# Swapped operands in the state-space output products, transposed outputs for the GLU, and an earlier load of the third token tile, in a one-core hybrid encoder step

## The chip, the cores and the metric

The kernel runs on 1 core of one Trainium2 chip. The metric is the device time of one execution in microseconds (us). The time before is 1225.95 us, the median of 3 runs (1225.14 to 1464.7 us).

## The reference

One layer of a streaming encoder runs over 2048 prompt frames (one new stream) and 8 x 16 frames of running streams, that is 17 tiles of 128 tokens with 1024 features, in float32:

```
z = rms_norm(x) @ w_in                      # [u | g_s | q | k | v | g_a], 6 x 512 columns
# state-space branch: 32 groups of 16 channels, each with 64 complex states
h[l] = a * h[l-1] + b @ u[l]
y    = gelu(Re(c @ h) + d * u)              # 512 channels
val, gate = split(y @ w_glu)
y_s  = val * sigmoid(gate)                  # the GLU
# attention branch: 8 heads of 64, own 64-frame chunk and 8 chunks before (prompt),
# or 512 cached frames (running streams)
y_a  = attention(rms_norm(q), rms_norm(k), v)
out  = x + concat[y_s * silu(g_s), y_a * silu(g_a)] @ w_out
```

Outputs are both token blocks, the newest keys and values, and the last states.

## The kernel before, in words

The program is written in an order fixed by hand. A foreground (`inproj`, `glu`, `outproj`) holds the large products; each step of it is one `mm3`: three 128x512 matmuls (high and low halves of split operands, lines 189 to 191) that add into one PSUM tile. After each step the foreground yields a cost, and `run` gives a share of it (`ratio`) as credit to a background (`s5`, then `decode`, then `attention`), whose pieces so fall between the foreground's steps on every engine's queue. Every DMA discussed here is issued by SyncE (SP), whose queue is strictly in order.

`inproj` makes three passes over the 17 tiles (u and k; v and q; the two gates). For each tile, `dma_h` loads the transposed tokens into `xraw`, which has one buffer; `conv_h` turns it into a high part `hhi` on ScalarE (line 228) and a low part `hlo` on VectorE (line 231), and only then is the next `xraw` load issued (line 214). At the start the first two tiles come in quarters (lines 349 to 354), the first 16 weight chunks are converted (`conv_w`), and each conversion issues the load of the weight chunk five ahead into a ring of five buffers (`load_w`, line 139). The third tile is loaded by `dma_h(2)` on line 370, behind all of these.

`s5` works in 8 batches of 4 groups. The tokens are cut into 272 runs of L = 8 positions (256 of the prompt, 16 of the running streams). For each batch, `UT` holds the inputs with (position in the run, channel) on partitions and the 272 runs along the free axis, and `HP` holds the state before each run. `step_b1` makes the state inputs (one 128x272 matmul per group, line 771), VectorE does the rotations and the scan, and `step_c` makes the outputs: for the blocks of 128, 128 and 16 runs it takes `UT` and `HP` as the stationary operand and the matrices `Tm` and `CA` as the moving one (lines 842 and 843, for the small block 849 and 852). The result has runs on partitions; a GELU on ScalarE reorders it, and `step_y` stores it to the DRAM tensor `y_d` (line 862: tokens by channels, three DMAs per batch in pieces of 256 bytes). `build_e` writes the next `Tm` with 8 small DMAs (line 701), and `load_u` loads `U` (line 711).

`glu` reads `y_d` one token tile at a time (`glu_load`, line 1336). `glu_tr` turns it with four transposes on TensorE (line 1344) and makes the high and low parts from PSUM (lines 1347 and 1348); they are the stationary operands of 24 matmuls per tile. The transposes stand in TensorE's queue in the middle of the tile before.

Of the kernel before, what the change touches and what calls it, by code (L numbers as in the profile page):

```python
# [7 lines left out]
F32 = mybir.dt.float32  # L8
# [11 lines left out]
L = 8  # L20
# [15 lines left out]
def rv(ap):  # L36
    return ap.bitcast(F32R)


# [4 lines left out]
class Build:  # L44
# [15 lines left out]
    def consts(self, st):  # L60
# [6 lines left out]
        self.y_d = d.tile([NT * 128, 512], F32, name="y_d")  # L67
# [14 lines left out]

        self.identr = c.tile([128, 128], F32R, name="ident")
        self.ident = fv(self.identr)
        nc.vector.tensor_scalar(self.identr, ip, 0.0, None, op0=OP.is_equal)
# [26 lines left out]
    def open_fg(self, st):  # L112
# [10 lines left out]
        for f in (1, 0):  # L123
            self.chunks += [((3, f, k), I["w_glu"][128 * k:128 * k + 128, 512 * f:512 * f + 512], None) for k in range(4)]
# [17 lines left out]
    def conv_w(self):  # L142
# [50 lines left out]
    def inproj(self):  # L193
# [176 lines left out]
        dma_h(2)  # L370
# [17 lines left out]
        for ps in range(3):  # L388
            for ti, t in enumerate(TILES):
# [5 lines left out]
                for gi in range(2):  # L395
                    g = passes[ps][gi]
                    z = self.psm.tile([128, 512], F32, tag="mm", name="z")
                    for k in range(8):
# [10 lines left out]
                        if ps == 2 and last and gi == 1 and k == 3:  # L409
                            self.glu_tr(TILES[0])  # L410
                            self.glu_load(TILES[1])
# [37 lines left out]
    def s5(self):  # L449
# [254 lines left out]
        y4 = self.y_d.rearrange("(c j) e -> c j e", j=L)  # L704
        BLK = [(0, 128), (128, 128), (256, 16)]
        U, P, UT, HP = {}, {}, {}, {}
# [15 lines left out]
        def step_a(b, i):  # L722
            c0, n = BLK[i]
            if i == 0:
                UT[b] = mp.tile([128, GB, 272], F32, tag="UT", name="UT")
                HP[b] = mp.tile([128, GB, 273], F32, tag="HP", name="HP")
                nc.vector.memset(HP[b][:, :, 0:1], 0.0)
                nc.vector.tensor_copy(HP[b][:, :, 257:273].rearrange("p g (b k) -> p g b k", k=2)[:, :, :, 0],
                                      h0[:, b * GB:(b + 1) * GB, :])
# [4 lines left out]
            nc.scalar.activation(out=UT[b][:, :, c0:c0 + n], in_=p[:, :, 0:n], func=AF.Copy)  # L734
# [39 lines left out]
        def step_swap(b, g):  # L774
            v = VV[b, g]
            vs = mp.tile([128, 256], F32, tag="vs", name="vs")
            nc.scalar.activation(out=vs[0:64], in_=v[64:128, 0:256], func=AF.Copy)
            nc.scalar.activation(out=vs[64:128], in_=v[0:64, 0:256], func=AF.Copy)
            if g == 0:
                SV[b] = mp.tile([128, GB, 2 * NB], F32, tag="sv", name="sv")  # L780
            nc.scalar.activation(out=SV[b][:, g], in_=v[:, 256:272], func=AF.Copy)
            VV[b, g] = v, vs

        def step_rot(b, g):
# [6 lines left out]
            tt(t1, co, v[:, 0:256], op=OP.mult)  # L791
# [12 lines left out]
        def step_h(b, g):  # L804
# [6 lines left out]
            tt(HP[b][:, g, 1:257], t3, t4, op=OP.subtract)  # L811

        def step_fin(b):
# [8 lines left out]
            h1 = HP[b][:, :, 257:273].rearrange("p g (b k) -> p g b k", k=2)[:, :, :, 1]  # L822
# [9 lines left out]
            nc.vector.tensor_copy(FINp[:, gs], HP[b][:, :, 256])  # L832

        def step_c(b, i):
            c0, n = BLK[i]
            p = ps.tile([128, GB, 128], F32, tag="y", name="y", bufs=2)
            y = mp.tile([128, L, GB * CH], F32, tag="y", name="y")
            yg = y[0:n].rearrange("p j (g h) -> p g j h", g=GB)
            ca = [CA[b][:, g, 1:9].rearrange("p j h -> p (j h)") for g in range(GB)]
            if i < 2:  # L840
# [4 lines left out]
            else:  # L845

                o = [p[32 * g:32 * g + n, 0] for g in range(GB)]
                for g in range(GB):
                    nc.tensor.matmul(o[g], UT[b][:, g, c0:c0 + n], Tm[b % 2][:, g], start=True, stop=False,
                                     tile_position=(0, 32 * g))  # L850
                for g in range(GB):
                    nc.tensor.matmul(o[g], HP[b][:, g, 257:257 + n], ca[g], start=False, stop=True,
                                     tile_position=(0, 32 * g))
                for g in range(GB):
                    nc.scalar.activation(out=yg[:, g], in_=o[g].rearrange("p (j h) -> p j h", j=L),
                                         func=AF.Gelu_apprx_tanh)
            YS[b, i] = y
# [16 lines left out]
        for n in range(3):  # L874
# [3 lines left out]
            if n == 0:  # L878
                build_c(0)
# [3 lines left out]
        for b in range(NBATCH):  # L883
            nx = b + 1 < NBATCH
            for sl in range(6):
# [7 lines left out]
                if b and 1 <= sl < 4:  # L893
                    step_y(b - 1, sl - 1)
# [8 lines left out]
                if b and sl < 3:  # L903
                    step_c(b - 1, sl)
# [18 lines left out]
        for i in range(3):  # L923
            step_c(NBATCH - 1, i)
            yield 1740
            step_y(NBATCH - 1, i)
# [680 lines left out]
```

## Time and profile before

| what | value |
| --- | --- |
| median of the runs shown | 1225.95 us |
| the profiled execution's own time | 1226.13 us |
| its span, first to last instruction | 1224.3 us |
| mean granted TensorE clock | 0.995 |
| VectorE busy | 742.6 us (61%) |
| ScalarE busy | 597.7 us (49%) |
| GpSimd busy | 366.6 us (30%) |
| DMA, mean over the span | 193 GB/s, 190119 packets |

The span is cut into stages that overlap: input projection until about 700 us (the state-space branch in its background from about 245 to 585 us, the cached attention until about 670 us), the GLU until about 880 us, and the output projection to the end; band attention runs behind the last two. Matmuls are pipelined, so a matmul's own duration (0.39 us for 128x512) is longer than the step from its start to the next one's; costs on TensorE are read from start to start. In the timeline an `x2` or `x16` counts instructions merged into one row; a product of two plain float32 operands is two instructions.

### The profile page before, as it was taken

How to read it: one execution, taken by the hardware profiler on the slowest of the kernel's cores; microseconds unless marked ns; L12 is line 12 of the kernel's file. 1: busy time of each engine (PE TensorE's matmuls, PEld its weight loads, DVE VectorE, ACT ScalarE, POOL GpSimd, SP SyncE). 2: the span in 40 equal slices, each digit the busy share in tenths (PEclk: the TensorE clock that was granted, in tenths of full speed). 3: DMA queues.
4: the chain of work that ended last, by engine and by line, in shares of the span. 5: the costliest groups of instructions: out<-in, count | busy, mean ns of one | idle time of the engine just before them, and what ended most of it. 6: DMA issues, size and time to landing. Idle time of an engine off the chain costs nothing.

```text
span 1224.3 us, 18936 instructions
## 1 busy us (share of the span) xinstructions
PE 1193.0 (97%) x6687; PEld 983.1 (80%) x6687; DVE 742.6 (61%) x1391; ACT 597.7 (49%) x1159; POOL 366.6 (30%) x455
## 2 busy tenths in 40 slices
PE   8999999899999998999999999999999999999998
PEld 5788888777788876887777878788888888888876
DVE  5324556868999988985444456565565555555511
ACT  6434446266666656553232346565654555455410
POOL 2433242557767735540000011111211121121120
PEclk9999999999999998999999999999999999999999
DMA  8876556655545567433895688897877777767243
GB/s 252 262 250 181 155 177 202 195 142 129 149 123 151 135 195 214 110 93 88 270 382 171 204 247 245 255 265 205 217 221 215 206 240 241 196 205 225 73 136 107
DMA packets 190119, 236.58 MB, mean 193 GB/s; under 512 B 58136, under 2 KB 122656, under 8 KB 189000
## 3 DMA queue, kind: packets, MB, share of 16 engines
q1 hardware_dynamic: 189016, 232.15, 64.2%
q0 software_dynamic: 864, 3.21, 0.8%
q8 instruction: 53, 0.87, 0.3%
q14 instruction: 42, 0.34, 0.1%
q10 hardware_dynamic: 144, 0.00, 0.0%
HBM read 169.48 MB, written 67.80 MB: 194 GB/s over the span
## 4 chain that ended last, share of the span: by engine, by line
PE 78%; DMA 6%; DVE 6%; POOL 3%; ACT 3%; issue 2%; SPq 1%; DVEq 0%; ACTq 0%; POOLq 0%
PE z L189 19%; PE z L191 18%; PE z L190 18%; PE o L1218 6%; PE pt L1200 5%; PE s L1170 5%; DMA wraw<-in_w_in_dram 3%; PE pt L294 1%; PE o L1057 1%; PE y L843 1%; SPq L701 1%; PE y L842 1%; PE v L771 1%; ACT whi L155 1%; PE s L1015 1%
## 5 line engine op out<-in xcount | busy, mean ns | idle before, releaser
L189 PE MATMUL z<-whi,hhi 128*128 128x512 f32 x816 | 339.2, 416 | 1.4 <-ACT whi L155 0.7
L190 PE MATMUL z<-wlo,hhi 128*128 128x512 f32 x816 | 321.3, 394 | 3.3 <-DVE wlo L156 3.1
L191 PE MATMUL z<-whi,hlo 128*128 128x512 f32 x816 | 320.7, 393 | 0.5 <-DVE hlo L231 0.5
L189 PEld LDWEIGHTS z<-whi,hhi 128*128 128x128 f32 x816 | 154.1, 189 | 38.9 <-issue 5.1
L190 PEld LDWEIGHTS z<-wlo,hhi 128*128 128x128 f32 x816 | 154.5, 189 | 36.5 <-DVE wlo L156 8.0
L191 PEld LDWEIGHTS z<-whi,hlo 128*128 128x128 f32 x816 | 154.0, 189 | 34.3 <-DVE hlo L231 1.0
L1207 ACT ACTIVATE pth<-pt 128x640 fp32r<-128x640 f32 (+4 forms) x128 | 81.7, 639 | 129.3 <-PE pt L1200 89.4
L1208 DVE TENSOR_TENSOR ptl<-pt,pth 128x640 fp32r<-128x640 f32 (+4 forms) x128 | 94.6, 739 | 60.6 <-ACT pth L1207 59.7
L189 PE MATMUL z<-whi,mh 128*128 128x512 f32 x272 | 113.7, 418 | 0.0
L1115 POOL MEMSET bias<- 64x64 f32 x32 | 4.7, 146 | 363.5 <-DMA bias<-tl_d 250.0
L1189 ACT ACTIVATE sn<-sn,mn 128x640 f32<-128x640 f32 (+4 forms) x128 | 96.9, 757 | 29.5 <-DVE mn L1180 29.4
L191 PE MATMUL z<-whi,ml 128*128 128x512 f32 x272 | 107.1, 394 | 1.3 <-POOL ml L1415 1.3
L190 PE MATMUL z<-wlo,mh 128*128 128x512 f32 x272 | 106.7, 392 | 0.0
L1180 DVE CUSTOM_DVE_ANT_0 sn<-s,bias 128x640 f32<-128x640 f32 (+4 forms) x128 | 93.3, 729 | 11.4 <-PE s L1170 10.4
L1170 PE MATMUL s<-ks,q 128*128 128x320 f32 (+1 forms) x448 | 87.4, 311 | 0.0
L1200 PE MATMUL pt<-ident,sn 128*128 128x128 f32 x560 | 83.0, 274 | 3.9 <-DVE ptl L1208 3.1
L1170 PEld LDWEIGHTS s<-ks,q 128*128 128x128 f32 x448 | 74.7, 188 | 11.1 <-DVE mn L1180 1.2
L1200 PEld LDWEIGHTS pt<-ident,sn 128*128 128x128 f32 x560 | 64.9, 140 | 22.5 <-ACT sn L1189 10.0
L231 DVE TENSOR_TENSOR hlo<-xraw,hhi 128x1024 fp32r<-128x1024 f32 x49 | 60.9, 1242 | 20.7 <-ACT hhi L228 20.6
L280 POOL TENSOR_SCALAR s<-s 128x8 f32<-128x8 f32 x34 | 15.9, 468 | 182.9 <-DVE s L279 182.3
L1228 DVE TENSOR_TENSOR ot<-o,tmp 64x512 f32<-64x512 f32 x32 | 22.0, 689 | 74.5 <-ACT tmp L1226 74.5
L191 PEld LDWEIGHTS z<-whi,ml 128*128 128x128 f32 x272 | 51.0, 188 | 13.2 <-POOL ml L1415 1.7
(268 smaller groups left out, 2171.3 us busy)
## 6 DMA issues: line engine op xcount, KB each, us to landing
xraw<-in_xT_dram SPq DMA_DIRECT2D x49, 512.0 KB, 4.5
q<-qt_d SPq DMA_DIRECT2D x64, 256.0 KB, 8.6
ks<-kt_d SPq DMA_DIRECT2D x28, 512.0 KB, 5.6
vhl<-vp_d SPq DMA_DIRECT2D x28, 512.0 KB, 6.7
wraw<-in_w_in_dram SPq DMA_DIRECT2D x48, 256.0 KB, 4.5
bias<-tl_d SPq DMA_DIRECT2D x32, 320.0 KB, 6.3
mt<-mt_d SPq DMA_DIRECT2D x17, 512.0 KB, 7.4
x<-in_x_dram SPq DMA_DIRECT2D x34, 256.0 KB, 5.8
```

The lines of the kernel that those rows point to most:

```text
L189: mm(z, a, whi, start=first, stop=False)
L190: mm(z, a, wlo, start=False, stop=False)
L191: mm(z, b, whi, start=False, stop=last)
L231: nc.vector.tensor_sub(lo, raw, fv(hi))
L1170: nc.tensor.matmul(ps_s[:, bank, 0:wp], Q[n, x2][:, s, 128 * a:128 * a + 128], KS[n][:, s, c0:c0 + wp], start=(x2 == 0), stop=(x2 == 1))
L1180: nc.vector.tensor_tensor_reduce(out=o, in0=i0, in1=i1, scale=1.0, scalar=3e38, op0=OP.add, op1=OP.min, accum_out=mn)
L1189: nc.scalar.activation(out=sn[:, 0:w], in_=sn[:, 0:w], func=AF.Exp, scale=-1.0, bias=mn, accum_out=SUM[n][:, a, s:s + 1])
L1200: nc.tensor.transpose(t[:, k], pr[:, 128 * k:128 * k + 128], self.ident)
L1207: nc.scalar.activation(out=h, in_=t[:, 0:w], func=AF.Copy)
L1208: post.append(lambda: nc.vector.tensor_tensor(out=l, in0=t[:, 0:w], in1=fv(h), op=OP.subtract))
L1218: nc.tensor.matmul(o[:, a0:a1], VB[n][:, j, s, :], t[:, 3 * a0 + j + a0:4 * (a1 - 1) + j + 1:4], start=(y == 0 and j == 4), stop=(y == 1 a ...
L1228: post.append(lambda: nc.vector.tensor_tensor(out=ot[mine], in0=o[mine], in1=tmp[mine], op=OP.add))
```

## The change

- `step_c` takes one group at a time and swaps the operands: `Tm` and `CA` are stationary, and `UT` and `HP` move with all 272 runs at once. The output has (position, channel) on partitions. The 16 runs of the running streams move to the front of `HP` and `UT` (`COL`), so that the 272 columns of `HP` are in one piece.
- `step_y` stores a batch with eight DMAs, one for each position in the run; a DMA has 16 partitions with 68 pieces of 16 floats (64 bytes) each. `y_d` is now [4, 16, 8, 17, 128]: channel block, channel in the group, group, token tile, token.
- `glu_load` therefore gets channels on partitions (pieces of 512 bytes). `glu_conv` takes the place of `glu_tr`: no transposes, the high and low parts are made from SBUF, and the rows of `w_glu` are loaded in the order of the channels.
- At the start `dma_h(2)` is called one place earlier, and the weight chunks from the 16th on are not loaded by the conversions there but by deferred calls from the 40th step on.
- One more yield stands in the prologue of `s5`; the yields beside the removed transposes are gone.

```
         self.W[key] = (hi, lo)
         if self.step:
             self.defer(self.T_LW, lambda: self.load_w(n + self.NR))
+        elif n + self.NR < 16:
+            self.load_w(n + self.NR)
         else:
-            self.load_w(n + self.NR)
+            self.defer(40 + 10 * (n + self.NR - 16), lambda: self.load_w(n + self.NR))
...
             for _ in range(4):
                 self.conv_w()
-        dma_h(2)
+            if j == 0:
+                dma_h(2)
...
-        def step_c(b, i):
-            c0, n = BLK[i]
-            p = ps.tile([128, GB, 128], F32, tag="y", name="y", bufs=2)
...
-                for g in range(GB):
-                    nc.tensor.matmul(p[0:n, g], UT[b][:, g, c0:c0 + n], Tm[b % 2][:, g], start=True, stop=False)
-                    nc.tensor.matmul(p[0:n, g], HP[b][:, g, c0:c0 + n], ca[g], start=False, stop=True)
-                nc.scalar.activation(out=yg, in_=p[0:n].rearrange("p g (j h) -> p g j h", j=L), func=AF.Gelu_apprx_tanh)
...
-        def step_y(b, i):
-            c0, n = BLK[i]
-            y = YS.pop((b, i))
-            nc.sync.dma_start(y4[c0:c0 + n, :, b * GB * CH:(b + 1) * GB * CH], y[0:n])
+        def step_c(b, g):
+
+            if g == 0:
+                YS[b] = mp.tile([128, GB, 272], F32, tag="y", name="y", bufs=1)
+            p = ps.tile([128, 272], F32, tag="y", name="y", bufs=2)
+            nc.tensor.matmul(p, Tm[b % 2][:, g], UT[b][:, g], start=True, stop=False)
+            nc.tensor.matmul(p, CA[b][:, g, 1:9].rearrange("p j h -> p (j h)"), HP[b][:, g, 0:272],
+                             start=False, stop=True)
+            nc.scalar.activation(out=YS[b][:, g], in_=p, func=AF.Gelu_apprx_tanh)
+
+        def step_y(b):
+
+            y = YS.pop(b)
+            o0 = (b // 2) * CH * 8 * NT * 128 + (b % 2) * 4 * NT * 128
+            for j in range(L):
+                nc.sync.dma_start(ap_of(self.y_d, o0 + 16 * j, [[8 * NT * 128, CH], [128, GB * NT], [1, 16]]),
+                                  y[16 * j:16 * j + 16].rearrange("p g (t c) -> p (g t) c", c=16))
...
-                if b and 1 <= sl < 4:
-                    step_y(b - 1, sl - 1)
+                if b and sl == 3:
+                    step_y(b - 1)
...
-                if b and sl < 3:
-                    step_c(b - 1, sl)
+                if b:
+                    for g in ((0,), (1,), (2, 3), (), (), ())[sl]:
+                        step_c(b - 1, g)
...
     def glu_load(self, t):
         y = self.ev.tile([128, 512], F32, tag="zs", name="y")
-        self.nc.sync.dma_start(y, self.y_d[128 * t:128 * t + 128])
+        self.nc.sync.dma_start(y.rearrange("p (k x) -> p k x", k=4),
+                               self.y_d[:, :, :, (t + 1) % NT].rearrange("k h g x -> (h g) k x"))
         self.GY[t] = y
 
-    def glu_tr(self, t):
+    def glu_conv(self, t):
+
         nc = self.nc
-        y = self.GY.pop(t)
-        pt = self.pst.tile([128, 4, 128], F32, tag="tr", name="ty")
-        for k in range(4):
-            nc.tensor.transpose(rv(pt[:, k]), rv(y[:, 128 * k:128 * k + 128]), self.identr)
+        y = self.GY.pop(t).rearrange("p (k j c) -> p k c j", k=4, j=L)
         hi = self.hp.tile([128, 8, 128], F32R, tag="hhi", name="yh")
         lo = self.hp.tile([128, 8, 128], F32R, tag="hlo", name="yl")
-        nc.scalar.activation(out=hi[:, 0:4], in_=pt, func=AF.Copy)
-        self.defer(1, lambda: nc.vector.tensor_tensor(out=lo[:, 0:4], in0=pt, in1=fv(hi[:, 0:4]), op=OP.subtract))
+        h4, l4 = (v[:, 0:4].rearrange("p k (c j) -> p k c j", j=L) for v in (hi, lo))
+        nc.scalar.activation(out=h4, in_=y, func=AF.Copy)
+        self.defer(1, lambda: nc.vector.tensor_tensor(out=l4, in0=y, in1=fv(h4), op=OP.subtract))
         self.GY[t] = hi, lo
```

The order of instructions moves in three places that matter here. First, TensorE at the first output products of the first batch (`y` is the output's PSUM tile, `T_2120` is one of the two `Tm`, `z` a foreground product). Before:

```order
L191 MATMUL z<-whi,hlo 128x512
L842 MATMUL y<-T_2120,UT 128x128
L843 MATMUL y<-CA,HP 128x128
L842 MATMUL y<-T_2120,UT 128x128
L843 MATMUL y<-CA,HP 128x128
L842 MATMUL y<-T_2120,UT 128x128
L843 MATMUL y<-CA,HP 128x128
L842 MATMUL y<-T_2120,UT 128x128
L843 MATMUL y<-CA,HP 128x128
L189 MATMUL z<-whi,hhi 128x512
```

and in the changed kernel (its lines 190 to 192 are the foreground's three matmuls, 774 is the state input):

```order
L192 MATMUL z<-whi,hlo 128x512
L842 MATMUL y<-UT,T_2120 128x272
L843 MATMUL y<-HP,CA 128x272
L190 MATMUL z<-whi,hhi 128x512
L191 MATMUL z<-wlo,hhi 128x512
L192 MATMUL z<-whi,hlo 128x512
```

A block of eight 128-column products has become one pair of 272 columns; three more pairs follow in the same batch.

Second, the DMA queue of SP at the stores of the first batch (`y_d<-y`), with the token load `xraw`, the state-space input loads `U` and the stores of queries and values (`qt_d`, `vp_d`) around them. Before:

```order
L244 DMA vp_d<-vhl 128x1024
L862 DMA y_d<-y 1024x1x64 x2
L244 DMA qt_d<-kt 64x8x128 x2
L214 DMA xraw<-in_xT_dram 128x1024
L862 DMA y_d<-y 128x1x64
L711 DMA U<-u_d 128x8x64
```

and in the changed kernel:

```order
L245 DMA vp_d<-vhl 128x1024
L245 DMA qt_d<-kt 64x8x128
L852 DMA y_d<-y 16x68x16 x8
L245 DMA qt_d<-kt 64x8x128
L215 DMA xraw<-in_xT_dram 128x1024
L714 DMA U<-u_d 128x8x64
```

Three stores at two places have become eight in a row, ahead of a query store and the next token load.

Third, the same queue at the start (`wraw` are weight chunks, `xtok` the third tile's plain tokens). Before:

```order
L139 DMA wraw<-in_w_in_dram 128x512 x14
L214 DMA xraw<-in_xT_dram 128x1024
L206 DMA xtok<-in_x_dram 128x1024
L244 DMA u_d<-plain 128x512 x2
L214 DMA xraw<-in_xT_dram 128x1024
```

and in the changed kernel:

```order
L137 DMA wraw<-in_w_in_dram 128x512 x9
L215 DMA xraw<-in_xT_dram 128x1024
L207 DMA xtok<-in_x_dram 128x1024
L245 DMA u_d<-plain 128x512 x2
L215 DMA xraw<-in_xT_dram 128x1024
```

Five weight loads no longer stand between the last needed chunk and the third tile.

## Rows read from the trace of the kernel before

**Rows 1.** Page, part 1: busy time, share of the span, instructions.

```profile
PE 1193.0 (97%) x6687; PEld 983.1 (80%) x6687; DVE 742.6 (61%) x1391; ACT 597.7 (49%) x1159; POOL 366.6 (30%) x455
```

**Rows 2.** Timeline of TensorE, state-space stage: start us, us, engine, line, operation.

```profile
292.67 0.39 PE L191 MATMUL z<-whi,hlo 128*128 128x512 f32 x1
292.89 0.38 PE L842 MATMUL y<-T,UT 128*128 128x128 f32 x2
...
294.91 0.39 PE L190 MATMUL z<-wlo,hhi 128*128 128x512 f32 x1
...
295.61 0.39 PE L190 MATMUL z<-wlo,hhi 128*128 128x512 f32 x1
295.84 0.39 PE L191 MATMUL z<-whi,hlo 128*128 128x512 f32 x1
296.07 0.62 PE L771 MATMUL v<-UT,VB 128*128 128x272 f32 x2
...
296.75 0.39 PE L190 MATMUL z<-wlo,hhi 128*128 128x512 f32 x1
...
304.07 0.40 PE L191 MATMUL z<-whi,hlo 128*128 128x512 f32 x1
304.40 0.41 PE L849 MATMUL y<-T,UT 128*16 128x128 f32 x8
...
305.29 0.40 PE L190 MATMUL z<-wlo,hhi 128*128 128x512 f32 x1
```

**Rows 3.** Timeline of TensorE at the first two tiles of the GLU.

```profile
701.69 0.40 PE L191 MATMUL z<-whi,hlo 128*128 128x512 f32 x1
...
702.53 0.40 PE L190 MATMUL z<-wlo,hhi 128*128 128x512 f32 x1
...
706.18 0.39 PE L191 MATMUL z<-whi,yl 128*128 128x512 f32 x1
...
707.92 0.51 PE L1344 MATMUL ty<-ident,y 128*128 128x128 f32 x4 [1.35 <-DMA y<-y_d]
...
708.57 0.40 PE L190 MATMUL z<-wlo,yh 128*128 128x512 f32 x1
```

**Rows 4.** Timeline of TensorE where the third token tile is first used.

```profile
34.00 0.39 PE L191 MATMUL z<-whi,hlo 128*128 128x512 f32 x1
...
35.72 0.50 PE L191 MATMUL z<-whi,hlo 128*128 128x512 f32 x1 [0.53 <-DVE hlo L231]
36.05 0.40 PE L189 MATMUL z<-whi,hhi 128*128 128x512 f32 x1
```

**Rows 5.** Timeline of SP's queue at the start.

```profile
12.43 16.07 SPq L139 DMA_DIRECT2D wraw<-in_w_in_dram  x14
28.55 0.43 SPq L214 DMA_DIRECT2D xraw<-in_xT_dram  x1
```

**Rows 6.** Windows: a batch's time, the GLU; busy us (instructions), clock, DMA share, GB/s.

```profile
371.00:408.00 37.00, 37.00 (x209) 30.08 (x209) 33.29 (x57) 23.54 (x54) 28.77 (x32) 1.00 0.55 138
710.00:880.00 170.00, 166.00 (x981) 142.26 (x981) 100.12 (x227) 100.03 (x225) 29.10 (x47) 1.00 0.83 239
```

**Rows 7.** Windows: one 256-byte store alone; tail of a load in 64-byte pieces.

```profile
565.00:565.50 0.50, 0.50 (x4) 0.40 (x3) 0.00 (x0) 0.50 (x1) 0.00 (x0) 1.00 1.00 211
592.75:593.00 0.25, 0.25 (x2) 0.19 (x2) 0.25 (x1) 0.00 (x0) 0.00 (x0) 1.00 0.69 64
```

**Rows 8.** Issues on SP's queue by line: ns min/median/max.

```profile
L862 SPq DMA_DIRECT2D y_d<-y x24: 525/590/1437, 296.9 to 576.6; - x24
L982 SPq DMA_DIRECT2D qbd<-qsd x2: 584/2044/3503, 589.1 to 589.7; - x2
```

**Rows 9.** Page, part 6: token load, from issue to landing in us.

```profile
xraw<-in_xT_dram SPq DMA_DIRECT2D x49, 512.0 KB, 4.5
```

**Rows 10.** Timeline: a token load's issue (SP) and its first use (ScalarE).

```profile
315.92 0.34 SPq L214 DMA_DIRECT2D xraw<-in_xT_dram  x1
...
324.35 1.06 ACT L228 ACTIVATE hhi<-xraw 128x1024 fp32r<-128x1024 f32 x1
```

More of the change, by code (lines that the diff above doesn't have):

```diff
@@ L33, in fv @@
     return ap.bitcast(F32)
-def rv(ap):
-    return ap.bitcast(F32R)
 def ap_of(t, offset, pat):
@@ L66, in consts @@
         self.u_d = d.tile([NT * 128, 512], F32, name="u_d")
-        self.y_d = d.tile([NT * 128, 512], F32, name="y_d")
+        self.y_d = d.tile([4, CH, 8, NT, 128], F32, name="y_d")
         self.kt_d = d.tile([4, 2, 64, 2, 2048], F32, name="kt_d")
@@ L81, in consts @@
         nc.gpsimd.iota(ip, pattern=[[1, 128]], base=0, channel_multiplier=-1)
-        self.identr = c.tile([128, 128], F32R, name="ident")
-        self.ident = fv(self.identr)
-        nc.vector.tensor_scalar(self.identr, ip, 0.0, None, op0=OP.is_equal)
+        self.ident = c.tile([128, 128], F32, name="ident")
+        nc.vector.tensor_scalar(self.ident, ip, 0.0, None, op0=OP.is_equal)
         self.nhalf = c.tile([128, 8], F32, name="nhalf")
@@ L123, in open_fg @@
         for f in (1, 0):
-            self.chunks += [((3, f, k), I["w_glu"][128 * k:128 * k + 128, 512 * f:512 * f + 512], None) for k in range(4)]
+            self.chunks += [((3, f, k), I["w_glu"][128 * k:128 * k + 128, 512 * f:512 * f + 512]
+                             .rearrange("(g h) c -> h g c", h=CH), None) for k in range(4)]
         for f in (0, 1):
@@ L733, in step_a @@
                 nc.tensor.transpose(p[:, g, 0:n], o[0:n, g], self.ident[0:n, 0:n])
-            nc.scalar.activation(out=UT[b][:, :, c0:c0 + n], in_=p[:, :, 0:n], func=AF.Copy)
+            nc.scalar.activation(out=UT[b][:, :, COL[i]:COL[i] + n], in_=p[:, :, 0:n], func=AF.Copy)
         def feed(n):
@@ L776, in step_swap @@
             vs = mp.tile([128, 256], F32, tag="vs", name="vs")
-            nc.scalar.activation(out=vs[0:64], in_=v[64:128, 0:256], func=AF.Copy)
-            nc.scalar.activation(out=vs[64:128], in_=v[0:64, 0:256], func=AF.Copy)
+            nc.scalar.activation(out=vs[0:64], in_=v[64:128, 16:272], func=AF.Copy)
+            nc.scalar.activation(out=vs[64:128], in_=v[0:64, 16:272], func=AF.Copy)
             if g == 0:
                 SV[b] = mp.tile([128, GB, 2 * NB], F32, tag="sv", name="sv")
-            nc.scalar.activation(out=SV[b][:, g], in_=v[:, 256:272], func=AF.Copy)
+            nc.scalar.activation(out=SV[b][:, g], in_=v[:, 0:16], func=AF.Copy)
             VV[b, g] = v, vs
@@ L790, in step_rot @@
             G = mp.tile([128, 256], F32, tag="G", name="G")
-            tt(t1, co, v[:, 0:256], op=OP.mult)
+            tt(t1, co, v[:, 16:272], op=OP.mult)
             tt(t2, si, vs, op=OP.mult)
@@ L810, in step_h @@
             tt(t4, si, Gs, op=OP.mult)
-            tt(HP[b][:, g, 1:257], t3, t4, op=OP.subtract)
+            tt(HP[b][:, g, 17:273], t3, t4, op=OP.subtract)
         def step_fin(b):
@@ L831, in step_fin @@
             tt(FINs[:, :, gs].rearrange("p b g -> p g b"), x8, y8, op=OP.add)
-            nc.vector.tensor_copy(FINp[:, gs], HP[b][:, :, 256])
-        def step_c(b, i):
-            c0, n = BLK[i]
-            p = ps.tile([128, GB, 128], F32, tag="y", name="y", bufs=2)
[L837 to L840, printed above, removed]
-                for g in range(GB):
-                    nc.tensor.matmul(p[0:n, g], UT[b][:, g, c0:c0 + n], Tm[b % 2][:, g], start=True, stop=False)
-                    nc.tensor.matmul(p[0:n, g], HP[b][:, g, c0:c0 + n], ca[g], start=False, stop=True)
-                nc.scalar.activation(out=yg, in_=p[0:n].rearrange("p g (j h) -> p g j h", j=L), func=AF.Gelu_apprx_tanh)
[L845 to L857, printed above, removed]
@@ L878, in s5 @@
             if n == 0:
+                yield SL
                 build_c(0)
@@ L922, in s5 @@
                     pass
[L923 to L926, printed above, removed]
+        for g in range(GB):
+            step_c(NBATCH - 1, g)
+            yield 1300
+        step_y(NBATCH - 1)
         pf = ps.tile([32, 128], F32, tag="ut", name="pf")
@@ L1383, in glu @@
                         if i + 1 < NT:
-                            self.glu_tr(TILES[i + 1])
-                            yield 430
+                            self.glu_conv(TILES[i + 1])
                         else:
```

11 lines of the change are left out of this document (6 added, 5 removed).

## The prediction

> **What bounds the kernel now.** I read the page's first part first: TensorE is busy for 97% of the span, every other engine for 61% or less [rows 1]. Busy time alone does not prove a bound, since matmuls overlap, so I then went through TensorE's timeline from start to start. Neighbouring foreground matmuls start 0.23 us apart (295.61 and 295.84 in [rows 2]), and this step is met nearly everywhere; the larger gaps are few, and two of them lie in the change's way [rows 3, 4]. The other engines matter only where TensorE waits for them. So whatever leaves TensorE's queue shortens the run one for one, unless another engine or SP's queue then comes too late. [...]
>
> **The output products.** For a stretch between two foreground matmuls I take the time from the last one before to the second one after and subtract two steps of 0.23 us (the first one after starts early, so it alone would mislead). A block of 128 runs: 294.91 - 292.67 - 0.46 = 1.78 us. The block of 16 runs: 305.29 - 304.07 - 0.46 = 0.76 us. A batch costs 2 x 1.78 + 0.76 = 4.32 us. The new shape, one 128x272 product of plain float32 operands, is in the trace already, as the state input on line 771: 296.75 - 295.84 - 0.46 = 0.45 us [rows 2]. A batch needs 4 groups x 2 = 8 of them, 3.60 us. The saving is 0.72 us per batch, 5.8 us for eight. Bounds: a product may cost 0.05 us more or less where two stand back to back, 64 x 0.05 = 3.2 us either way.
>
> **The GLU's transposes.** At the first tile they cost 702.53 - 701.69 - 0.46 = 0.38 us [rows 3]; 17 tiles make 6.5 us, all of it on TensorE. Between attention pieces I could not separate them as cleanly; 0.30 to 0.45 us per tile gives 5.1 to 7.7 us. At the second tile the same stretch is 708.57 - 706.18 - 0.46 = 1.93 us, because the transposes stand in TensorE's queue waiting for the load of `y` (1.35 us idle). In the changed kernel ScalarE waits there instead, and the result is needed by TensorE only at the next tile, some 24 matmuls later; this gives another 1.93 - 0.38 = 1.55 us. The high and low parts now read SBUF with a stride instead of PSUM: still 512 elements a partition. I cost that at nothing, since in this stage VectorE and ScalarE are each busy 100 of 170 us [rows 6]; without this cover 17 reads made longer by a half microsecond would be 8.5 us. The loads of 512-byte pieces are issued a tile ahead.
>
> **The third tile.** TensorE goes from 34.00 to 36.05 over four steps that should take 0.92 us: 1.13 us lost, to the low part of the third tile [rows 4]. Its load is issued at 28.55 because fourteen weight loads stand before it, 16.07 us of SP's queue [rows 5]. In the new order only nine do; five fewer of some 1.1 us bring the load about 5.7 us forward, much more than the wait. So I take 1.1 us. The five weight loads come later by single issues; their chunks are converted only at the end of the first pass, so the price is nothing.
>
> **The stores.** A batch had 272 x 8 = 2176 pieces of 256 bytes and now has 8 x 16 x 68 = 8704 of 64 bytes, 544 per DMA engine instead of 136. No 64-byte store is in the trace. One side of the bound is a load in 64-byte pieces: its tail moves 64 GB/s at a share of 0.69 [rows 7], 93 GB/s at a full share, or 64 bytes in 11 ns per engine. The other is the old store: 211 GB/s at a share of 1.00, 256 bytes in 19.4 ns. A batch's stores then hold the engines for 544 x 11 = 6.0 us to 544 x 19.4 = 10.6 us, against 136 x 19.4 = 2.6 us. The share of 0.55 in this stage [rows 6] leaves room: 8 us more at most in the some 37 us of a batch (eight of them have their stores between 296.9 and 576.6 [rows 8], 280 us for somewhat more than seven periods). The order is the danger. Eight issues of 0.59 us are 4.7 us, and SP can be held longer when many pieces are queued: the second load in 64-byte pieces took 3.50 us to issue [rows 8]. Behind them stand a query store and a token load. A token load needs 4.5 us to land [rows 9], and from 315.92 to its first use at 324.35 there are 8.4 us [rows 10], so 3.9 us to spare in this instance. Between the bounds ScalarE could wait 6.0 - 3.9 = 2.1 to 10.6 - 3.9 = 6.7 us in a batch whose token load follows directly. TensorE uses that tile only one tile later, and has a second PSUM buffer for what ScalarE clears meanwhile. So the loss lies between 0 and 8 x 6.7 = 54 us. I take 2 us, near the lower end, since the 64-byte load is the nearer row.
>
> [...]
>
> **Sum.** From the profiled execution's own 1226.13 us: - 5.8 - 6.5 - 1.55 - 1.1 + 2 = 1213.2, taken as 1213.0 us. The profiled execution is within 0.2 us of the median of the runs shown, so the same number stands for that median.
>
> **Rivals.**
>
> *The stores hold the queue (slower).* If 64-byte stores cost as much as 256-byte ones, or more, and the token load stands right behind them in half of the batches, ScalarE waits 6.7 us in four of them, and if TensorE sees all of it the time is 1211.2 + 27 = 1238 us. At twice that price per piece (21 us a batch) it is 1211.2 + 4 x 17 = 1279 us. It decides against the change when more than 15 us are lost, that is from 3.7 us in four batches. For it: the order, and the 3.50 us issue [rows 8]. Against it: the store wait is shared with a tile of lead, and the engines are half free [rows 6]. [...] I give the rival 0.12, of which 0.06 lies above 2%.
>
> *VectorE becomes the bound in the state-space stage.* It is busy 33.29 of 37 us there [rows 6]; with TensorE 0.72 us shorter a batch, its waits could take back the 5.8 us: 1219 us. Against it: 3 us a batch are still free. 0.14.
>
> *The change does not do what it says at the start.* If the weights, not the tile, set TensorE's pace to 36 us, 1.1 us stay: 1214 us, inside the forecast's own range.
>
> *More than that.* ScalarE's GELU comes in four pieces instead of six, and freed waits could add up to the 6 us by which the bounds above exceed my terms: 1207 us. 0.06.
>
> **How the numbers follow.** The forecast has 0.68 (1209 to 1217 us). The range must leave out no more than 0.2: it takes in the case above it at 1219, the lower one at 1207 and the milder half of the slow rival, so 1206 to 1230 us. About 2% is what a measurement of this kernel can tell from no change, 24.5 us. Faster by more needs 1201 or less, which no case reaches: 0.03. Slower by more is the harder half of the slow rival: 0.06. The rest is 0.91.
>
> **What would show it.** Right: line 842 and 843 with 64 products each (128 instructions each), a pair costing 0.9 us between foreground matmuls; no transposes in the GLU and no wait for `y` at its start; the third tile's load issued near 23 us and TensorE in step from 34 us on. Wrong: ScalarE waiting for `xraw` between 300 and 580 us, SP's store issues far above 0.59 us, or new TensorE waits on VectorE in that stretch. The prediction is wrong if the state-space stage is longer than before.

## The result and the profile after

| | before | after |
|---|---|---|
| median of the runs, us | 1226.59 (8 runs) | 1232.27 (8 runs) |
| lowest and highest, us | 1223.22, 1228.04 (one of 1464.7 left aside) | 1228.48, 1236.52 |
| ratio, with its 95% interval | | 1.0051 [1.0031, 1.007] |
| profiled execution, its span, us | 1226.13, 1224.3 | 1231.64, 1229.6 |

Predicted were 1213.0 us in a range of 1206 to 1230. The change makes the kernel half a per cent slower: too little to count as slower by 2%, and outside the range.

Part 1 of the page, in place of [rows 1]:

```profile
PE 1186.3 (96%) x6363; PEld 973.0 (79%) x6363; DVE 747.9 (61%) x1391; ACT 600.5 (49%) x1143; POOL 364.7 (30%) x455
```

TensorE is busy 6.7 us less with 324 instructions fewer, and the run is still longer. So it waits more, and the question is where.

What was to become cheaper did. TensorE's timeline in the state-space stage, a pair of the new output products between foreground matmuls (as [rows 2]):

```profile
291.91 0.39 PE L192 MATMUL z<-whi,hlo 128*128 128x512 f32 x1
292.14 0.62 PE L842 MATMUL y<-UT,T 128*128 128x272 f32 x2
292.60 0.62 PE L843 MATMUL y<-HP,CA 128*128 128x272 f32 x2
...
293.29 0.40 PE L191 MATMUL z<-wlo,hhi 128*128 128x512 f32 x1
```

293.29 - 291.91 - 0.46 = 0.92 us for two products, as forecast. SP's queue at the start, against [rows 5]:

```profile
12.46 10.38 SPq L137 DMA_DIRECT2D wraw<-in_w_in_dram  x9
22.89 0.42 SPq L215 DMA_DIRECT2D xraw<-in_xT_dram  x1
```

The third tile's load goes out 5.7 us earlier, and TensorE's wait of [rows 4] is gone: nine steps from 34.16 to 36.20 us take 2.04 us, 0.23 us each.

```profile
34.16 0.39 PE L192 MATMUL z<-whi,hlo 128*128 128x512 f32 x1
...
36.20 0.39 PE L192 MATMUL z<-whi,hlo 128*128 128x512 f32 x1
```

To place the loss I counted foreground matmuls in both timelines and compared the times at which the 841st (211.8 us before, ahead of the state-space stage), the 2401st (693.8, ahead of the GLU) and the 3481st (1174.2, after the attention) start. The table gives what each stretch gained (-) or lost (+) against the kernel before, in us. One profiled run each: the untouched state-space stage of start_only shows that about 2 us are chance.

| kernel | start | state-space and decode | GLU, attention |
|---|---|---|---|
| after | -1.7 | +0.9 | +8.4 |
| start_only | -1.4 | -1.9 | -1.2 |
| s5_only | -0.2 | -0.7 | +5.9 |
| glu_only | 0.0 | -2.0 | +9.6 |
| plain_read | -1.1 | +0.3 | +3.7 |
| ms01_dve | -0.9 | +3.1 | +1.7 |
| plain_ms01 | -2.2 | +0.7 | +2.1 |
| long_store | -1.4 | -3.1 | +9.8 |
| plain_ms01_long | -1.7 | -4.8 | -2.0 |
| one_prod | -1.7 | +1.2 | +9.1 |
| dve_less | -1.5 | -2.0 | +6.0 |
| order_store | -1.6 | +0.8 | -0.1 |

So the start gave what was promised, the state-space stage gave nothing, and the stretch with the GLU, where 8 us were to be gained, lost 8. The last column also nets a shift: without the yields beside the transposes, some 50 of the attention's matmul instructions (426 against 476 between the 2401st and the 2809th foreground matmul) leave the GLU and run behind it. The GLU alone is 0.8 us longer although it holds less, and what follows it is 7.6 us longer.

In the GLU three things stand in the trace. First, ScalarE's copy and VectorE's subtraction that read `y` with a stride (one line's instructions: ns min/median/max):

```profile
L1340 ACT ACTIVATE yh<-y x17: 1082/1097/1117, 702.3 to 873.8; 128x512 fp32r<-128x512 f32 x17
L1341 DVE TENSOR_TENSOR yl<-y,yh x17: 1007/1054/1564, 704.6 to 874.9; 128x512 fp32r<-128x512 f32 x17
```

Before they took medians of 598 and 686 ns from PSUM:

```profile
L1347 ACT ACTIVATE yh<-ty x17: 592/598/603, 702.4 to 873.3; 128x512 fp32r<-128x512 f32 x17
L1348 DVE TENSOR_TENSOR yl<-ty,yh x17: 680/686/692, 704.2 to 873.9; 128x512 fp32r<-128x512 f32 x17
```

Second, among TensorE's waits between 690 and 900 us (total, times, longest):

```profile
PE pt L1193 <- DVE ptl L1201: 6.0, 6, 1.5
PE tm L1352 <- POOL ms L1392: 4.9, 1, 4.9
PE z L192 <- DVE yl L1341: 1.1, 1, 1.1
```

The first two of these waits in the kernel before were

```profile
PE pt L1200 <- DVE ptl L1208: 2.7, 5, 0.9
PE tm L1359 <- POOL ms L1400: 1.2, 1, 1.2
```

The attention's transposes (line 1193) wait for VectorE, whose queue has become longer. The 4.9 us are one stall, on TensorE's timeline:

```profile
727.20 0.38 PE L1193 MATMUL pt<-ident,sn 128*128 128x128 f32 x2
732.47 1.11 PE L1352 MATMUL tm<-ident,ms 128*128 128x128 f32 x4 [4.89 <-POOL ms L1392]
```

Third, what holds GpSimd, on its timeline:

```profile
713.39 0.15 POOL L1108 MEMSET bias<- 64x64 f32 x1 [3.32 <-DMA bias<-tl_d]
...
713.70 1.28 POOL L1392 TENSOR_TENSOR ms<-ms,gs 128x512 f32<-128x512 f32 x1
730.85 0.15 POOL L1108 MEMSET bias<- 64x64 f32 x1 [15.87 <-DMA bias<-tl_d]
...
731.16 1.25 POOL L1392 TENSOR_TENSOR ms<-ms,gs 128x512 f32<-128x512 f32 x1
```

and on SP's:

```profile
708.36 0.50 SPq L1107 DMA_DIRECT2D bias<-tl_d  x1
708.90 0.43 SPq L329 DMA_DIRECT2D gs_d<-plain  x1
715.01 0.32 SPq L1366 DMA_DIRECT2D gs<-gs_d  x1
...
717.12 2.60 SPq L1127 DMA_DIRECT2D q<-qt_d  x4
719.76 0.58 SPq L1107 DMA_DIRECT2D bias<-tl_d  x1
```

with SP's longest wait for that product between 700 and 740 us

```profile
SPq L1366 <- POOL ms L1392: 4.8, 1, 4.8
```

Read together it is a chain. GpSimd clears the corners of a bias tile when it has landed (713.39), and the gate product of the first tile stands behind that in its queue, until 714.98. SP stands at a gate's load until 715.01, and by its waits it is that product (4.8 us) that it stands for. What follows on SP is late: the next bias goes out at 719.76, behind four query loads. GpSimd waits for it until 730.85, 11 us later, and the second tile's product, which stands behind that and whose input VectorE had finished at 722.4, comes at 731.16. TensorE needs it at 727.6. In the kernel before this bias went out at 716.84 and GpSimd cleared it at 725:

```profile
716.84 0.58 SPq L1114 DMA_DIRECT2D bias<-tl_d  x1
```

```profile
724.99 0.15 POOL L1115 MEMSET bias<- 64x64 f32 x1 [8.81 <-DMA bias<-tl_d]
```

After the stall TensorE also runs slower (windows: busy us, then granted clock, DMA share, GB/s):

```profile
727.20:732.50 5.30, 0.41 (x4) 0.17 (x2) 0.51 (x3) 0.38 (x1) 1.51 (x3) 0.82 1.05 327
732.50:738.00 5.50, 5.50 (x18) 4.53 (x19) 1.39 (x3) 1.54 (x4) 0.36 (x3) 0.55 0.65 217
```

Having been idle for 4.9 us, TensorE is granted 0.55 over the next 5.5 us: 0.50 until 736.5 us, and 1.00 again from 737.5 us. By the granted clock that is an estimated 5.5 x 0.45 = 2.5 us more.

### The profile page after: what moved, and what is told of

It is laid out like the page before. It is cut to its first block, busy times and chain, and to the rows that moved or that the text cites. A ratio compares the mean times of both kernels' runs of the same rounds, so it can differ in the third digit from the quotient of the medians.

```text
span 1229.6 us, 18291 instructions
## 1 busy us (share of the span) xinstructions
PE 1186.3 (96%) x6363; PEld 973.0 (79%) x6363; DVE 747.9 (61%) x1391; ACT 600.5 (49%) x1143; POOL 364.7 (30%) x455
## 4 chain that ended last, share of the span: by engine, by line
PE 68%; DMA 10%; DVE 9%; SPq 5%; ACT 4%; issue 3%; POOL 1%; DVEq 0%; ACTq 0%; POOLq 0%
PE z L190 16%; PE z L192 15%; PE z L191 15%; PE o L1211 5%; PE pt L1193 5%; PE s L1163 5%; DMA wraw<-in_w_in_dram 3%; SPq L852 2%; SPq L703 1%; DVE hlo L232 1%; DMA bias<-tl_d 1%; PE o L1050 1%; PE pt L295 1%; DMA gs_d<-plain 1%; PE y L843 1%
## 5 line engine op out<-in xcount | busy, mean ns | idle before, releaser
L282 POOL TENSOR_TENSOR s<-s,nhalf 128x8 f32<-128x8 f32 x34 | 61.6, 1811 | 2.9
```

The costliest lines, as they stand in the source:

```text
L282: nc.gpsimd.tensor_tensor(out=s8, in0=s8, in1=self.nhalf, op=OP.pow)
```

## The experiments

Results, with the ratio to the kernel before on the same chip (medians in us; the changed kernel had 1.0051). The kernels ran on several chips, so differences between them go by the ratios, times 1226 us.

| kernel | median, runs | ratio [95%] |
|---|---|---|
| start_only | 1224.01, 12 | 0.9981 [0.9966, 0.9997] |
| s5_only | 1234.27, 6 | 1.0074 [1.0047, 1.010] |
| glu_only | 1233.09, 6 | 1.0062 [1.0044, 1.0081] |
| plain_read | 1225.73, 12 | 0.9998 [0.9986, 1.0011] |
| ms01_dve | 1224.85, 12 | 1.0002 [0.9986, 1.0018] |
| long_store | 1226.65, 12 | 1.0009 [0.9994, 1.0023] |
| plain_ms01 | 1221.63, 11 | 0.9964 [0.9949, 0.998] |
| plain_ms01_long | 1215.20, 6 | 0.9918 [0.990, 0.9936] |
| one_prod | 1227.70, 12 | 1.0014 [0.9994, 1.0034] |
| dve_less | 1227.88, 11 | 1.0010 [0.9999, 1.0021] |
| ms01_spread | 1227.78, 12 | 1.0001 [0.9979, 1.0022] |
| ms01_actq | 1285.98, 6 | 1.0484 [1.0452, 1.0517] |
| perm | 1232.63, 6 | 1.0062 [1.004, 1.0083] |
| perm_ms01 | 1227.40, 12 | 1.0013 [0.9992, 1.0033] |
| order_store | 1222.66, 12 | 0.9962 [0.9946, 0.9979] |
| order_all | 1222.99, 12 | 0.9970 [0.9951, 0.9989] |
| order_yield | 1227.06, 12 | 1.0010 [0.9989, 1.0031] |
| start_ms01 | 1223.07, 12 | 0.9973 [0.9955, 0.9991] |

**Each part alone.** The parts of the change's own diff, put one at a time into the kernel before.

start_only: 

> The kernel before with the start alone: third token tile loaded after the first tile's weights, weight loads from the sixteenth on by single issues. The two traces put the after kernel 1.7 us ahead from matmul 120 on, and this lead is still 1.8 us at the end of the state-space stage. Theory 'the lead is the start's': 1.7 us faster than before, about 1224.9 us, ratio 0.9986. Rival 'a lead at the start is eaten by the next wait on another engine': no difference, ratio 1.000.

s5_only: 

> The kernel before with the state-space part alone (operands swapped, 64-byte stores in eight pieces a batch); the GLU keeps its loads and its transposes, so its input is y in another order. Theory 'waits eat the gain': TensorE's work falls by 5 us, waits rise by as much, ratio 1.000 (1226 to 1228 us). Rival 'the stores hold SP's queue and cost more than the products save': 1230 us or more, ratio over 1.003. Rival 'the stage gains, and what was lost is the GLU's alone': 1221 us, ratio 0.996.

glu_only: 

> The kernel before with the GLU part alone: no transposes of y, the high and low parts read y from SBUF with a stride, loads in 512-byte pieces, rows of the weights in the new order; the state-space stage stores as before, so the GLU's input is y in another order. Theory 'the GLU is what loses': 6 us slower than before although 6.5 us of TensorE's work are gone, 1232 us, ratio 1.005. Rival 'the GLU gains as forecast and the loss needs the state-space part too': 1219 us, ratio 0.994.

The start's edit is a gain of 0.2% (2.3 us). Either of the other parts by itself makes the kernel slower, by 0.6 to 0.7%. The parts don't add up: 2.3 less, 9.1 more and 7.6 more would make 14 us more, and the whole change costs 6. In glu_only the attention's transposes wait 10.0 us (9 times) for VectorE between 690 and 900 us, against 2.7 us before, which fits its loss in the last column. For s5_only the table of stretches shows no loss in its own stage but 5.9 us in the GLU and the attention, which are not edited there; the cause was not found, and its profiled run (1229.12 us) was 5 us faster than its median, so the rest of its loss is not seen.

**The strided read.**

```
-  y = self.GY.pop(t).rearrange("p (k j c) -> p k c j", k=4, j=L)
-  h4, l4 = (v[:, 0:4].rearrange("p k (c j) -> p k c j", j=L) for v in (hi, lo))
+  y = self.GY.pop(t).rearrange("p (k x) -> p k x", k=4)
+  h4, l4 = hi[:, 0:4], lo[:, 0:4]
```

plain_read: 

> The changed kernel with high and low parts of y read in storage order, one unbroken run of 512 elements, so that tokens within a tile stay in another order; all else as in the changed kernel. Theory 'the strided read is the cost': ScalarE's copy falls from 1.0 us to 0.6, VectorE's subtraction from 0.93 or more to 0.6, and the GLU's waits go; 8 to 14 us faster than the changed kernel, 1218 to 1224 us, ratio 0.993 to 0.998. Rival 'the stall behind GpSimd's product is one of order, not of the read': ScalarE and VectorE faster but 1230 to 1233 us, ratio 1.003 to 1.005.

The same two lines in plain_read:

```profile
L1340 ACT ACTIVATE yh<-y x17: 614/622/632, 701.2 to 869.4; 128x512 fp32r<-128x512 f32 x17
L1341 DVE TENSOR_TENSOR yl<-y,yh x17: 684/693/1389, 703.0 to 870.0; 128x512 fp32r<-128x512 f32 x17
```

The stride costs ScalarE 0.48 us and VectorE 0.36 us a tile, and the kernel 6.5 us. TensorE's wait for `ptl` falls to

```profile
PE pt L1193 <- DVE ptl L1201: 2.1, 4, 0.9
```

while the stall behind GpSimd stayed (5.5 us in this run). In the changed kernel neighbouring elements of the read lie 64 bytes apart, here side by side, and the medians are 1097 against 622 ns on ScalarE and 1054 against 693 ns on VectorE.

**The chain behind GpSimd.**

```
+  if i < 2:
+      self.defer(1, lambda ms=ms, g=g: nc.vector.tensor_tensor(out=ms, in0=ms, in1=g, op=OP.mult))
+  elif i + 1 < NT:
-  if i + 1 < NT:
       self.defer(1, lambda ms=ms, g=g: nc.gpsimd.tensor_tensor(out=ms, in0=ms, in1=g, op=OP.mult))
```

ms01_dve: 

> The changed kernel with one edit: in the GLU's first two tiles the product with the gate (GpSimd, line 1392) is made by VectorE, so that it no longer stands behind GpSimd's memset of the bias, which waits for that bias to land. Theory 'the chain memset, product, gate load, SP makes the 5.1 us stall at 727 us': the stall and the halved clock behind it go, 6 to 9 us faster than the changed kernel, 1224 to 1226 us, ratio to before 0.998 to 1.000. Rival 'the attention's softmax on VectorE is late anyway (subtractions into ptl)': the stall moves to those, 1230 us or more, ratio over 1.003.

TensorE's timeline of ms01_dve has the first two transposes of the GLU's output without a wait:

```profile
720.23 0.60 PE L1352 MATMUL tm<-ident,ms 128*128 128x128 f32 x4
...
729.42 0.60 PE L1352 MATMUL tm<-ident,ms 128*128 128x128 f32 x4
```

The granted clock stays 1.00 in the windows 720 to 738 us, and the kernel is 6.0 us faster than the changed one, most of the stall and the clock behind it together (4.9 + 2.5 = 7.4). One link of the chain fell, though: SP stands at the gate's load until 716.22 here too, now for the landing of a store of the gate,

```profile
SPq L1366 <- DMA gs_d<-plain: 5.0, 1, 5.0
```

and the bias is still cleared only at 729.40. So the product's place behind the bias is what cost, not its hold on SP.

start_ms01 puts the same edit into start_only: 

> The kernel before with the start's edit and the first two gate products on VectorE. Theory 'the chain behind the bias is brought on by the change': before had at most 1.2 us of it at one tile, so as start_only, 1224 us, ratio 0.998. Rival 'the chain costs the kernel before too': 1218 to 1220 us, ratio 0.994.

0.9973 against 0.9981, with intervals that overlap: in the old order the chain costs next to nothing. The change brought it on. Which part of it did is not shown: at this tile glu_only has 1.8 us of the wait, s5_only at most 0.6 us, and the kernels with both parts and the product on GpSimd have 3.8 to 5.7 us.

plain_ms01: 

> The changed kernel with y read in storage order (as plain_read, tokens in another order) and the first two gate products on VectorE (as ms01_dve). Theory 'two separate causes in the GLU': gains of 6.5 and 7.4 us add up, 1218.5 us, ratio to before 0.994. Rival 'either edit merely shifts the same stall': 1225 us, ratio 0.9995.

0.9964 against a sum of 1.0051 - 0.0053 - 0.0049 = 0.9949: most of both gains is kept. In this run GpSimd's product stalled TensorE at a later tile instead (3.4 us at 776 us).

**The stores.**

```
-  nc.sync.dma_start(ap_of(self.y_d, o0 + 16 * j, [[8 * NT * 128, CH], [128, GB * NT], [1, 16]]),
-                    y[16 * j:16 * j + 16].rearrange("p g (t c) -> p (g t) c", c=16))
+  nc.sync.dma_start(ap_of(self.y_d, (128 * b + 16 * j) * GB * 272, [[GB * 272, CH], [1, GB * 272]]),
+                    y[16 * j:16 * j + 16].rearrange("p g x -> p (g x)"))
```

long_store: 

> The changed kernel with the eight stores of y a batch as before in number, but each in 16 pieces of 4352 bytes instead of 1088 of 64; so the GLU reads y in another order. Theory 'the short pieces hold SP's queue and the DMA engines, so that the T tables land late and VectorE waits for them (6.5 us in the changed kernel) and TensorE for VectorE': the state-space stage gets 4 us shorter, 1228 us, ratio 1.002. Rival 'the waits of that stage come from the new places of the products and of the GELUs among the instructions, whatever the stores are': 1231 to 1233 us as the changed kernel, ratio 1.005.

plain_ms01_long: 

> As plain_ms01, and the stores of y in pieces of 4352 bytes as in long_store. Theory 'three separate causes': 6.5 + 7.4 + 5.6 us under the changed kernel's 1232.3, 1213 us, ratio 0.990, which is the time that was forecast for the change without them. Rival 'long stores shift the GLU's stalls and are worth the 2 us that the state-space stage showed': 1216 to 1224 us, ratio 0.992 to 0.998.

SP's queue at one batch, first in the changed kernel:

```profile
377.77 7.35 SPq L852 DMA_DIRECT2D y_d<-y  x8
385.21 1.78 SPq L245 DMA_DIRECT2D qt_d<-kt  x2
387.59 1.11 SPq L215 DMA_DIRECT2D xraw<-in_xT_dram  x1
```

then in long_store:

```profile
376.95 3.57 SPq L852 DMA_DIRECT2D y_d<-y  x8
...
386.78 0.36 SPq L215 DMA_DIRECT2D xraw<-in_xT_dram  x1
```

Short pieces hold SP twice as long; over the eight batches of the changed kernel the hold is 7.3 to 9.0 us. They cost 5.1 us alone and 5.6 us beside the other two edits (6.4 us by the medians, on one chip). The table of stretches puts the gain where these stores are: the state-space stage is 4.0 us shorter than in the changed kernel, and 5.5 us shorter in plain_ms01_long than in plain_ms01. (The profiled run of long_store, 1229.23 us, was 2.6 us slower than its median.) With all three costs taken away the kernel takes 1215.2 us, the forecast within 3 us.

ms01_spread, four stores in each of two slots: 

> As ms01_dve, with the eight stores of a batch issued in two halves, four in the fourth and four in the fifth slot. Theory 'SP's queue held for 8 us in a row is what delays the loads behind it': 3 to 5 us less than ms01_dve, 1220 to 1222 us, ratio 0.996. Rival 'the number of short pieces costs, whenever they are issued': 1225 us, ratio 1.000.

ms01_actq, `nc.scalar.dma_start` for `nc.sync.dma_start`: 

> As ms01_dve, with the stores of y issued from ScalarE's queue instead of SP's. Theory 'SP's queue is what the short stores cost': SP has 8 us more a batch, 3 to 6 us less than ms01_dve, 1219 to 1222 us, ratio 0.995. Rival 'ScalarE, which the state-space stage needs, pays for the issues': eight issues of 1 us a batch in front of its copies, slower than ms01_dve, 1228 us or more, ratio over 1.002. Rival 'the DMA engines' time': 1225 us, ratio 1.000.

Splitting the eight issues gains nothing, which speaks against a long hold at one go as the cost. On ScalarE's queue the kernel takes 59 us more than the one before. Waits of ms01_actq between 290 and 620 us:

```profile
PE ut L736 <- ACT VB L681: 43.2, 6, 9.4
ACT VB L681 <- DMA y_d<-y: 40.5, 5, 9.0
```

ScalarE stands idle for 8.95 us while its queue issues six of these stores, and TensorE waits for ScalarE:

```profile
357.43 7.94 ACTq L852 DMA_DIRECT2D y_d<-y  x5
365.42 0.60 ACT L681 ACTIVATE VB<-pv 128x512 f32<-128x512 f32 x1 [8.95 <-DMA y_d<-y]
```

The edit that would tell SP's hold from the DMA engines' time has thus made a new wait. Which of the two costs the 5 to 6 us stays open.

**The state-space stage.**

one_prod, without the first matmul of line 842: 

> The changed kernel without the first product (T tables by input) of line 842: 32 products of 0.46 us between foreground matmuls, 14.7 us of TensorE's work in the state-space stage, are left out, and with them part of y. Theory 'that stage goes at the pace of VectorE and ScalarE': the stage loses under 4 us, 1228 us or more, ratio over 1.002. Rival 'TensorE bounds it and the eight places alone were bad': 14 us less, 1218 us, ratio 0.994.

dve_less, without the product of line 813: 

> The changed kernel without one of VectorE's three operations on each group's states (the product of line 813, left out of the computation): 32 x 0.42 = 13.4 us of VectorE's 246 us between 290 and 570 us. Theory 'VectorE sets the pace of the state-space stage': the waits for VectorE there go, 4 to 6 us less, 1226 to 1228 us, ratio 1.000 to 1.002. Rival 'TensorE bounds the stage': 1231 to 1233 us as the changed kernel, ratio 1.005.

Busy us of TensorE, weight loads, VectorE, ScalarE and GpSimd, clock, DMA share and GB/s from 290 to 570 us, and TensorE's wait for the rotated input. The changed kernel:

```profile
290.00:570.00 280.00, 269.87 (x1260) 214.78 (x1259) 245.96 (x416) 160.19 (x347) 156.77 (x180) 0.99 0.59 141
```

```profile
PE v L774 <- DVE t L794: 3.0, 4, 1.7
```

one_prod:

```profile
290.00:570.00 280.00, 262.48 (x1205) 205.29 (x1204) 245.78 (x419) 159.40 (x348) 156.98 (x180) 0.98 0.60 141
```

```profile
PE v L774 <- DVE t L794: 10.1, 6, 2.7
```

and dve_less:

```profile
290.00:570.00 280.00, 271.60 (x1268) 216.56 (x1267) 235.19 (x386) 159.07 (x347) 157.43 (x179) 0.99 0.59 141
```

The upper of each pair is the window, the lower the wait. 14.7 us of TensorE's work taken out bring 4.5 us, and TensorE's wait for VectorE grows from 3.0 to 10.1 us. VectorE's busy time is the same in both. (The profiled run of one_prod, 1232.56 us, was 4.9 us slower than its median; its stretch shows no gain in this stage at all, so in a usual run the waits take back less.) In dve_less 13.4 us of VectorE's work taken out bring 5.0 us, 2.9 us of them in this stage by the stretches. So neither engine bounds this stage alone: they hand work to each other, and either shortened by itself gives back about a third. Both runs keep the short stores.

**A version that keeps the gains.** perm reads plainly and puts the tokens right again where the transposes of the GLU's output write PSUM; the gate must then be in the same order.

```
-  nc.tensor.transpose(pt[:, k], ms[:, 128 * k:128 * k + 128], self.ident)
+  nc.tensor.transpose(pt[:, k].rearrange("p (c j) -> p j c", j=L), ms[:, 128 * k:128 * k + 128], self.ident)
...
-  nc.sync.dma_start(g, self.gs_d[128 * t:128 * t + 128])
+  nc.sync.dma_start(g, ap_of(self.gs_d, 128 * t * 512, [[512, L], [L * 512, 16], [1, 512]]))
```

perm: 

> The changed kernel with y read in storage order, as in plain_read, but with the right result: the gate's rows are loaded in the same order (2-KB pieces), and the transposes of the GLU's output write their columns to PSUM with a stride, which puts the tokens back. Theory 'the order of a tile costs nothing where a transpose can write it': as plain_read, 1225 to 1227 us, ratio to before 1.000. Rival 'the strided writes to PSUM cost TensorE what the strided reads cost the others': over 1229 us, ratio over 1.003; the four transposes of a tile would then take more than 0.38 us between foreground matmuls.

perm_ms01: 

> Both edits, of perm and of ms01_dve. Theory 'two separate causes': the gains add up, 1217 to 1220 us, ratio 0.994 to 0.996, and the 5.5 us stall at 726 us, which plain_read still had, is gone. Rival 'one gain takes the place of the other': 1224 to 1226 us, ratio 0.999.

order_store leaves that load plain and permutes the gate where it is stored, 17 times in the input projection, with 16 rows outermost: 

> As perm_ms01 (plain read, right result, strided writes of the transposes to PSUM), but the gate's rows are put into storage order when they are stored, so that its load is one plain block. Theory 'perm lost by the load of the gate in permuted rows, 0.62 us to issue and late to land': as plain_ms01, 1221 to 1223 us, ratio 0.996. Rival 'the strided writes to PSUM are what cost 6 us': as perm_ms01, 1227 us, ratio 1.001.

perm gave up the 6.5 us of the plain read. perm_ms01 and order_store, which differ only in where the gate is permuted, lie 6.3 us apart, and order_store is as fast as plain_ms01 (0.9962 and 0.9964), which permutes nothing. Since perm_ms01 and order_store both write PSUM with the stride, it was the load. The transposes have the same duration in order_store (first) and in the changed kernel (second):

```profile
L1353 PE MATMUL tm<-ident,ms x68: 270/272/329, 716.9 to 884.1; 128*128 128x128 f32 x68
```

```profile
L1352 PE MATMUL tm<-ident,ms x68: 270/273/473, 718.2 to 893.5; 128*128 128x128 f32 x68
```

Their ends are modelled, so the step counts more: between two foreground matmuls the four transposes cost 878.93 - 878.03 - 0.46 = 0.44 us in order_store and 884.85 - 883.95 - 0.46 = 0.44 us in ms01_dve, which writes plainly. The load took a median of 0.62 us to issue in perm against 0.38 in order_store; its landing is not recorded. Why this load costs the kernel some 6 us is not shown.

order_all, where the last tile's product, on VectorE already, is made twice: 

> As order_store, with the gate product of all 17 tiles on VectorE. Theory 'GpSimd's queue behind the biases costs in later tiles too': 2 to 3 us less than order_store, 1220 us, ratio 0.994. Rival 'VectorE has no room: 15 more operations of 0.69 us delay the softmax': 1224 us or more, ratio 0.998 or over.

order_yield: 

> As order_store, with the step of 430 put back behind each tile's conversion, so that the attention is served in the GLU as often as in the kernel before. Theory 'the attention that is put off in the GLU (some 50 of TensorE's instructions) comes back later at full price': no difference, 1222 to 1223 us, ratio 0.996. Rival 'served less, the attention ends late and its waits lie open at the end': 2 us less, 1220 us, ratio 0.994.

order_all is no different from order_store. order_yield is slower by 5.9 us (4.4 by the medians), which neither side expected. With the attention served more often inside the GLU, its transposes wait for VectorE 5.3 us (7 times) instead of 1.4 (4 times), but other waits there are shorter and the two profiles end the attention within 3 us of each other, so the cause is not shown. order_store beats both kernels, by 0.4% and 0.9%; start_only, one edit, has half of the gain over the kernel before.

## Why the prediction was wrong

*Output products (-5.8 us).* The size was right: 4 x 0.92 = 3.68 us a batch against 3.60 forecast. The stage gained nothing in the changed kernel, but with long stores it is 3.1 us shorter than before (long_store) and 4.8 us (plain_ms01_long), so the stores took back most of it. The rule above this step, "whatever leaves TensorE's queue shortens the run one for one, unless another engine or SP's queue then comes too late", is at its exception here: one_prod got 4.5 us for 14.7 us of TensorE's work, because TensorE then waits for VectorE (10.1 us against 3.0). The rival "VectorE becomes the bound" had this mechanism, at 0.14; against it stood the "3 us a batch" that 33.29 of 37 us [rows 6] leave free, but in one_prod TensorE waited for VectorE with VectorE busy 245.8 of 280 us. How much of the 5.8 us went that way is not shown, since one profiled run differs from another by about 2 us.

*Transposes in the GLU (-6.5 us) and the wait at its second tile (-1.55 us).* They are gone, with a wait of 1.1 us for `yl` at the first tile in place of the second. The step that failed is "I cost that at nothing", of the strided reads, because "VectorE and ScalarE are each busy 100 of 170 us". Half free on average was no cover: the attention's transposes waited for VectorE six times, up to 1.5 us each. The plain read cut TensorE's wait for `ptl` from 6.0 to 2.1 us. The strided one cost 6.5 us (plain_read), as much as the transposes had been forecast to save; the prediction's own price without cover, 8.5 us, was the better number.

*The chain behind GpSimd.* It is in no step. The prediction looked at SP's queue only for the start and the state-space stage, and did not ask how the loads of the attention move in the GLU, nor what stands behind GpSimd's wait for a bias. Its sum has no term for the clock; behind the stall of 4.9 us the granted clock fell to 0.55 over 5.5 us. Together 6.0 us (ms01_dve).

*The stores (+2 us).* The price of a piece was right, its effect was mis-sized. In the trace's single DMA packets the 64-byte pieces took 10.9 ns in the mean, 544 x 10.9 = 5.9 us a batch, the forecast's lower end. The shares agree: from 290 to 570 us the DMA share is 0.59 after, against 0.52 in the window of the kernel before:

```profile
290.00:570.00 280.00, 273.23 (x1496) 221.14 (x1496) 247.35 (x417) 164.83 (x362) 158.63 (x180) 0.99 0.52 140
```

0.07 x 280 / 7 batches = 2.8 us more a batch, with the forecast's 2.6 us for the old store some 5.4 us. ScalarE had no wait for a token load between 295 and 585 us in either kernel, so the way by which the forecast and the rival let the stores cost was wrong; which wait they lengthen instead is not shown. SP was held 7.3 to 9.0 us a batch instead of 4.7. The term measured 5.1 to 5.6 us (long_store, plain_ms01_long) where 2 were taken. The doubled price that the slow rival weighed (21 us a batch) does not show in that share.

*Third tile (-1.1 us).* Right in mechanism; 2.3 us alone, with an interval from 0.4 to 4.2 us.

From forecast to result it is 19.3 us. The strided read (6.5 us), the chain with the clock (6.0 us) and the stores (3.1 to 3.6 us beside the 2 that were taken) make some 16 of them. The rest is seen in plain_ms01_long, which lacks all three. Were all other terms right, it would reach the forecast's sum without the store term, 1211.2 us, which is 14.9 us less than before; it is 10.1 us less. Its state-space stage gains 4.8 us of the 5.8, but its GLU and attention 2.0 us of the 8.05; why the GLU gives no more is not shown. That its 1215.2 us lie so near the forecast's 1213.0 is partly luck: the 2 us for stores that it does not have stand in for some of that.

## What to carry to other kernels

When an operation leaves the busiest engine, price the work that replaces it at the place where the next one waits, not against the mean load of the engine that takes it over: 0.36 to 0.48 us more per tile on the two engines that also serve the attention cost as much as the four transposes were forecast to save. When a change shifts loads, follow every in-order queue through one round of the loop, and look what stands behind an instruction that waits for a transfer. If data must be reordered, let a transpose that is made anyway do it: here its strided write cost nothing (0.44 us for four either way).

## What the runs showed that was not expected

A strided write of the transposes to PSUM cost nothing (0.44 us for four with the stride and without), while the strided read from SBUF cost 0.36 to 0.48 us. Eight issues of short-piece stores a batch from ScalarE's queue made the kernel 59 us slower than before, and a step of 430 in a loop's pace cost 4.4 to 5.9 us.
